# Layer 0 of a hybrid backbone: attention gates made a pair of tiles ahead, constants and some split weights kept in DRAM between the phases

## The chip, the cores and the metric

The kernel runs on one core of a Trainium2 chip. The metric is the device time of one execution in microseconds (us), the median of several runs. The engines are TensorE (PE; its weight loads are shown as PEld), VectorE (DVE), ScalarE (ACT), GpSimd (POOL) and SyncE (SP), whose queue issues the DMAs.

## The reference, cut to what matters

A latent stream of 2048 tokens and a context of 256 tokens, both 1024 wide, go through two layers. Every layer is a pre-RMSNorm sub-layer with shift, scale and gate rows that come from a conditioning vector. Layer 0 has one input projection that feeds two branches, and one output projection:

```python
u, v, ga, q, k, vv, gb = _split(h @ w_in, AB_SIZES)
ya = chunk_gmlp(gelu(u), gelu(v), ln_g, ln_b, w_s, b_s) * silu(ga)
yb = window_attention(q, k, vv, kc, vvc, sink) * silu(gb)
y = concatenate([ya, yb], axis=-1) @ w_out
```

`chunk_gmlp` applies a group layer norm to v and mixes the 128 positions of a chunk with a 128 x 128 matrix for each of 4 groups (`w_s`), adds `b_s` and multiplies by u. The attention has windows of +-128 tokens, the context as a prefix and a sink. Layer 1 is a bidirectional RG-LRU: a convolution of width 4, block-diagonal gates with biases and a decay that contains softplus(-lam), one scan in each direction, a SiLU gate and an output projection. A last RMSNorm gives the output.

## The kernel before

There are 18 tiles of 128 tokens (2 of context, 16 of latents), in 9 pairs. All is float32. For matmuls every operand is split into a high part that PE takes in one pass and a low part, the rest (`split`: the high part by a copy, on ACT unless said otherwise, and the low part by a subtraction, on DVE unless said otherwise); `mm3` multiplies high by high, low by high and high by low. A weight "unit" is half of the contraction of a block of 512 columns, or all of it for 256 columns: 2 MB with both parts. It is loaded in two halves of 0.5 MB through `raws`, six buffers of 4 KB a partition, and split (`unit_halves`). A "kept" half (`keep_halves`) is loaded, split and stored in DRAM with both parts; later one transfer of 1 MB (`kept_half`) brings it ready.

The program has four parts, which follow each other on the engines' queues.

1. The attention stage, a loop of steps `s` over tiles (18 and three more for the pipeline to drain). Each step makes one tile's norm, its transposed h (stored in DRAM as `h0s`), q, k and v, and the scores, softmax and values of an earlier tile, in four quarter steps that `merge` interleaves. One piece of other work from the list `mg_at` goes into a quarter step, from quarter step MOD_AT on: pieces of the conditioning rows (`mod_half`, tiles mraw, macc and msum) and kept halves of layer 1's weights. The tail (`tail_q`), in the last three steps, computes some of the ga and v projections ahead and loads weights `wu` 2 to 4.
2. The projection phase (the block of `c2`): u and v of a tile (`part_v`, `part_u`: matmuls pvv and pu), layer norm, the spatial product of a pair (`pair_b`: matmuls sv, tile ub), stored as `yas`. At its start `consts` loads and transposes the spatial weights (wsT) and 92 rows of small constants (cv) on PE, and computes softplus (tiles spt and sps). Weights for the next phase are split along the way.
3. The output phase (the block of `c3`): for a pair of tiles, `gate_b` loads the attention's outputs (ot) and the pair's h (one buffer, hp3), computes the SiLU gate by 96 matmuls pg of 256 columns and makes ybT; `y_rows` loads ya and transposes it on DVE (yT, 128 blocks of 32 x 256 over the phase), and its split gives yaT. `out_a` computes the output of one tile by 48 matmuls po of 512 columns (first the 12 on yaT, then 12 on ybT, for either half), the residual (xt) and the next layer's norm; its `fin`, called one tile later, transposes the new rows on DVE (h1T; on PE from tile 14 on), modulates them and stores them as `h1s`.
4. Layer 1, whose order on PE, ACT and DVE is written out by hand.

In the first three parts the order on each engine's queue comes from a planner that simulates the program: what comes first in the program, or is marked with a high priority, goes first where it is ready by the planner's own times. Each engine then runs its queue in order. Buffers of a phase lie where those of the phase before it lay; a tile waits for the last reader of what it covers.

In the order of the program the output phase before reads as follows, with `yaT` in one buffer and `ybT` in two:

```python
gated = gate_b(0); rows = [y_rows(0)]
for pr in range(NPAIR):
    split(yaT...)                        # pair pr, low part on POOL but for pr 0
    if pr == 0: wo.extend(...)           # the last two output weights: load and split
    for x in range(2):
        f = out_a(2 * pr + x, yaT, ybT); if pend: pend(); pend = f
        if x == 0 and pr + 1 < NPAIR:
            gated = gate_b(pr + 1); rows.append(y_rows(pr + 1))
```

## Time and profile before

| what | value |
|---|---|
| median of 3 runs | 2016.53 us (2014.89 to 2018.07) |
| the profiled execution, its own time | 2019.23 us |
| its span, first to last instruction | 2017.4 us |
| mean granted TensorE clock | 0.974 of full speed |
| PE busy | 1903.2 us (94%) |
| DVE busy | 1527.7 us (76%) |
| ACT busy | 1086.5 us (54%) |
| POOL busy | 619.8 us (31%) |

Busy time of an engine is the time in which it executes an instruction; matmuls overlap, so that the time from start to start is what one costs, and not its duration. A row of waits names the waiting engine and tile, and behind the arrow what it waited for last. The chain of waits follows the work that ended last back from releaser to releaser. All times count from the first instruction. "Granted clock" is the share of PE's full clock (2.4 GHz) that the chip allowed; its lower level is half of that.

### The profile page before, as it was taken

What the parts mean: (1) busy time and instruction counts of PE and PEld (TensorE: products, weight loads), DVE (VectorE), ACT (ScalarE), POOL (GpSimd) and SP (SyncE); (2) the same over time, 40 slices, a digit from 0 to 9 for tenths busy, and PEclk for the clock granted to TensorE, in tenths of its full rate; (3) what the DMA queues carried; (4) which work ended last, traced back from release to release, by engine and by line L of the source; (5) the groups of instructions that cost most, each with busy time, mean ns of one, the idle gap of its engine ahead of it and who ended that gap; (6) DMA issues with size and microseconds to landing.
All of it is one profiled execution on the core that took longest, in us unless ns stands there. A gap on an engine that the chain in (4) does not pass through costs nothing.

```text
span 2017.4 us, 33905 instructions
## 1 busy us (share of the span) xinstructions
PE 1903.2 (94%) x12159; PEld 1701.9 (84%) x12159; DVE 1527.7 (76%) x3223; ACT 1086.5 (54%) x2205; POOL 619.8 (31%) x801
## 2 busy tenths in 40 slices
PE   7999999999999899799989999999999999988998
PEld 3778888888887788688878889999999999877777
DVE  8878989786745787838888854798987566877863
ACT  6656656666655332323443551676767666756621
POOL 2745646454422311200010010443422121244310
PEclk8999999999999899899999999999999999988999
DMA  9355535352344897465555555324476464866442
GB/s 344 124 180 186 176 137 176 118 199 71 126 142 149 297 353 281 172 230 182 198 205 182 206 208 186 107 100 147 167 260 222 161 200 167 295 218 192 136 160 91
DMA packets 184788, 375.79 MB, mean 186 GB/s; under 512 B 18694, under 2 KB 78858, under 8 KB 176428
## 3 DMA queue, kind: packets, MB, share of 16 engines
q1 hardware_dynamic: 184620, 373.64, 53.0%
q8 instruction: 95, 1.56, 0.3%
q14 instruction: 73, 0.60, 0.1%
HBM read 246.41 MB, written 127.17 MB: 185 GB/s over the span
## 4 chain that ended last, share of the span: by engine, by line
PE 57%; DVE 19%; ACT 10%; DMA 7%; issue 6%; POOL 1%; SPq 1%; POOLq 0%; DVEq 0%; ACTq 0%
PE px L90 6%; PE px L92 6%; PE px L91 6%; DVE h1T L904 4%; PE pu L90 3%; PE pu L91 3%; PE pu L92 3%; PE po L573 3%; PE ptp L561 2%; DVE yT L904 2%; DVE macc L231 2%; ACT h1T L175 2%; DMA mraw<-in_w_mod 2%; PE pl L515 1%; PE pq L91 1%
## 5 line engine op out<-in xcount | busy, mean ns | idle before, releaser
L90 PE MATMUL px<-op,w 128*128 128x256 f32 x1088 | 308.1, 283 | 0.0
L91 PE MATMUL px<-op,w 128*128 128x256 f32 x1088 | 307.9, 283 | 0.0
L92 PE MATMUL px<-op,w 128*128 128x256 f32 x1088 | 307.9, 283 | 0.0
L91 PEld LDWEIGHTS px<-op,w 128*128 128x128 f32 x1088 | 208.9, 192 | 0.0
L90 PEld LDWEIGHTS px<-op,w 128*128 128x128 f32 x1088 | 208.9, 192 | 0.0
L92 PEld LDWEIGHTS px<-op,w 128*128 128x128 f32 x1088 | 208.9, 192 | 0.0
L543 POOL TENSOR_SCALAR s<-s,ri 128x640 f32<-128x640 f32 (+2 forms) x144 | 134.4, 947 | 97.1 <-DVE ri L540 93.0
L535 ACT ACTIVATE s<-s,mn 128x641 f32<-128x641 f32 (+2 forms) x144 | 113.3, 788 | 65.8 <-DVE mn L517 57.7
L84 ACT ACTIVATE pT<-ptp 128x512 fp32r<-128x512 f32 (+1 forms) x192 | 99.7, 536 | 89.5 <-PE ptp L561 86.4
L1108 POOL TENSOR_TENSOR ig<-ig,zf 128x512 f32<-128x512 f32 x72 | 109.9, 1534 | 98.0 <-ACT ig L1106 88.7
L87 DVE TENSOR_TENSOR zhl<-zf,zhl 128x512 fp32r<-128x512 f32 x72 | 60.2, 843 | 102.8 <-ACT zhl L84 102.7
L573 PE MATMUL po<-pT,v 128*128 128x256 f32 x656 | 130.1, 296 | 6.1 <-DVE pT L87 4.4
L87 DVE TENSOR_TENSOR pT<-ptp,pT 128x512 fp32r<-128x512 f32 (+1 forms) x192 | 114.4, 604 | 23.3 <-ACT pT L84 22.6
L90 PE MATMUL px<-w,op 128*128 128x512 f32 x256 | 103.5, 404 | 14.9 <-ACT px L1240 14.9
L573 PEld LDWEIGHTS po<-pT,v 128*128 128x128 f32 x656 | 98.5, 189 | 17.2 <-DVE pT L87 9.1
L175 ACT ACTIVATE h1T<-h1T,mc 128x128 f32<-128x128 f32 x112 | 44.7, 482 | 119.0 <-DVE h1T L904 119.0
L561 PE MATMUL ptp<-ident,s 128*128 128x128 f32 x656 | 104.0, 273 | 3.9 <-POOL s L543 2.1
L1152 POOL COPY carry<-T 128x2 f32<-128x2 f32 x68 | 34.7, 510 | 232.1 <-DVE T L1149 222.1
L904 DVE STREAM_TRANSPOSE h1T<-hrow 32x256 f32<-32x256 f32 x224 | 97.7, 436 | 8.1 <-ACT hrow L956 5.0
L91 PE MATMUL px<-w,op 128*128 128x512 f32 x256 | 102.5, 400 | 0.0
L92 PE MATMUL px<-w,op 128*128 128x512 f32 x256 | 102.4, 400 | 0.0
L517 DVE CUSTOM_DVE_ANT_0 s<-pl,mask,mn 128x384 f32<-128x384 f32 (+1 forms) x128 | 76.1, 594 | 31.5 <-PE pl L515 30.1
(280 smaller groups left out, 6237.4 us busy)
## 6 DMA issues: line engine op xcount, KB each, us to landing
hp<-h0s SPq DMA_DIRECT2D x45, 1024.0 KB
op<-h1s SPq DMA_DIRECT2D x64, 512.0 KB
mraw<-in_w_mod SPq DMA_DIRECT2D x48, 512.0 KB
h0s<-hT SPq DMA_DIRECT2D x18, 1024.0 KB
h1s<-h1hl SPq DMA_DIRECT2D x36, 512.0 KB
xt<-in_x SPq DMA_DIRECT2D x32, 512.0 KB
gs<-gs SPq DMA_DIRECT2D x64, 256.0 KB
raw<-in_ab_w_in SPq DMA_DIRECT2D x22, 512.0 KB
```

The source lines that it names most:

```text
L84: act.activation(hi, src, AF.Copy)
L87: (eng_lo or dve).tensor_tensor(lo, src, hi.bitcast(F32), ALU.subtract)
L90: pe.matmul(ps, lhsT=lhs(0), rhs=rhs(0), start=first, stop=False)
L91: pe.matmul(ps, lhsT=lhs(1), rhs=rhs(0), start=False, stop=False)
L92: pe.matmul(ps, lhsT=lhs(0), rhs=rhs(1), start=False, stop=last)
L175: act.activation(hT[:, o], tp[:, i], AF.Identity, scale=mc[:, 1, k, m:m + 1], bias=mc[:, 0, k, m:m + 1])
L535: act.activation(s[:, 0:nk], s[:, 0:nk], AF.Exp, scale=-1.0, bias=st["mn"][:, row, i:i + 1], accum_out=st["sm"][:, i:i + 1])
L543: pool.tensor_scalar(s[:, 1:nk], s[:, 1:nk], ri[:, i:i + 1], 0.0, ALU.mult, ALU.add)
L561: pe.transpose(tp[:, x, h], s_t[h][:, 1 + i * P:1 + (i + 1) * P], ident)
L573: pe.matmul(pos[t, g][:, 2 * P * e:2 * P * (e + 1)], lhsT=vl, rhs=pT[:, hl, x], start=i == 0 and hl == 0, stop=i == n - 1 and hl == 1)
L904: dve.transpose(out[o, :, s], src[s, :, o])
L1108: pool.tensor_tensor(res[1], res[1], zfs.pop((d, i, b)), ALU.mult)
```

## The change

- Output phase: the gates of pair `pr + 1` are made in the program before both outputs of pair `pr` (before: between the two). The split of ya has its low part on DVE for every pair (before: on POOL but for the first); the rows of the pair after it are loaded and transposed behind the split. For the first pair the ya split comes first of all, and both its gates and those of the second pair come ahead of the first output. The second pair's h goes to four of the six raw buffers in eight transfers; the other pairs keep the one hp3 buffer.
- The output projection's last two weights (four halves) and weights 4 and 5 of the input projection (four halves) are split as kept halves in the attention stage and come ready by 1 MB transfers. Both before were loaded and split where they were needed (4 in the tail, 5 at the start of the projection phase).
- The constants (spatial weights, the 92 columns, softplus) are made in three pieces at the head of the attention stage's list of pieces, stored in DRAM, and loaded behind it by three transfers. The list begins two quarter steps earlier (MOD_AT 6) and has 63 pieces instead of 52; the kept halves are spread evenly in it.
- h of the first two tiles of the projection phase is loaded during the attention tail, into a weight buffer.

The diff, cut to its core:

```diff
@@ constants @@
-MOD_AT = 8
+MOD_AT = 6
@@ new, at the head of the program @@
+    wsd = dram.tile([P, 2, 4, P], F32, name="wsd")
+    cvd = dram.tile([P, 92], F32, name="cvd")
+    spd = dram.tile([P, 3, 16], F32, name="spd")
+    def const_pieces(bank):
+
+        st = {}
+
+        def spatial():
+            wsr = raws.tile([P, 4, P], F32, tag="raw", name="wsr")
+            sp.dma_start(wsr, a["a_w_s"][0].rearrange("g p q -> p g q"))
+            wsT = raws.tile([P, 2, 4, P], F32R, tag="raw", name="wsT")
+            tp = bank([P, 4, P], "wstp")
+            for g in range(4):
+                pe.transpose(tp[:, g], wsr[:, g], ident)
+            split(wsT[:, 0], wsT[:, 1], tp)
+            sp.dma_start(wsd, wsT.bitcast(F32))
...
+            tpc = bank([P, 92], "cvtp")
+            pe.transpose(tpc, cr, ident[0:92, 0:92])
+            v = st["v"] = raws.tile([P, 256], F32, tag="raw", name="cols")
+            dve.tensor_copy(v[:, 0:92], tpc)
...
+            sp.dma_start(spd, o)
+
+        return [spatial, columns, softplus_neg]
@@ attention stage @@
-                    w, st[0] = unit_halves(pool_, wu_cols(i), act, (pool, dve))
+                    if i < 4:
+                        w, st[0] = unit_halves(pool_, wu_cols(i), act, (pool, dve))
+                    else:
+                        w = pool_.tile([P, 2, KT // 2, 512], F32R, tag="w", name="w")
+                        st[0] = lambda h: kept_half(w, ("wu", i), h)
+        hp01 = []
+
+        def load_hp01():
+            hp01.append(wb0.tile([P, 2, 2, KT, P], F32R, tag="w", name="hp01"))
+            for t in range(2):
+                sp.dma_start(hp01[0][:, t].bitcast(F32), h0s[t])
+
+        tail_q.insert(len(tail_q) * 2 // 3, load_hp01)
...
+        keep = [lambda i=i, h=h: keep_halves(("wu", i), wu_cols(i), h) for i in range(4, 6) for h in range(2)] + keep
+        keep += [lambda i=i, h=h: keep_halves(("wo", i), wide(a["ab_w_out"][0], 512, i), h) for i in range(2) for h in range(2)]
+        mg = const_pieces(mod_bank)
         for n, group in enumerate(groups):
-            mg += group + keep[3 * n // 2:3 * (n + 1) // 2]
+            mg += group + keep[len(keep) * n // 8:len(keep) * (n + 1) // 8]
@@ projection phase @@
+    sp.dma_start(cv[:, 0:92], cvd)
+    sp.dma_start(sps, spd)
...
+        for t in range(2):
+            hps[t] = hp01[:, t]
+        w = next_w().tile([P, 2, KT // 2, 512], F32R, tag="w", name="w")
         with tc.high_priority():
-            load_h(0)
-        load_h(1)
-        wu = wus + [unit_w(wu_cols(5), act, (pool, pool))]
+            for h in range(2):
+                kept_half(w, ("wu", 5), h)
+        wu = wus + [w]
         part_g(0)
+        wsT = b1.tile([P, 2, 4, P], F32R, name="wsT")
+        sp.dma_start(wsT.bitcast(F32), wsd)
...
-            if t == 0:
-                wsT, bs = consts()
@@ output phase, gate_b @@
-            hp = b1.tile([P, 2, 2, KT, P], F32R, tag="hp3", name="hp3")
-            for x in range(2):
-                sp.dma_start(hp[:, x].bitcast(F32), h0s[2 * pr + x])
+            if pr == 1:
+                hps_ = []
+                for q in range(4):
+                    hps_.append(raws.tile([P, 2, 2, 2, P], F32R, tag="raw", name="hp3"))
+                    for x in range(2):
+                        sp.dma_start(hps_[q][:, x].bitcast(F32), h0s[2 * pr + x][:, :, 2 * q:2 * q + 2])
+
+                def rows_of(hl, k):
+                    return hps_[k // 2][:, :, hl, k % 2]
+            else:
+                hp = b1.tile([P, 2, 2, KT, P], F32R, tag="hp3", name="hp3")
+                for x in range(2):
+                    sp.dma_start(hp[:, x].bitcast(F32), h0s[2 * pr + x])
+
+                def rows_of(hl, k):
+                    return hp[:, :, hl, k]
...
-                            lambda hl: hp[:, :, hl, k], k == 0, k == KT - 1)
+                            lambda hl: rows_of(hl, k), k == 0, k == KT - 1)
@@ output phase, the loop @@
+        def y_halves(raw, lo):
+            yaT = b1.tile([P, 2, 2, 4, P], F32R, tag="yaT3", name="yaT3")
+            split(yaT[:, 0], yaT[:, 1], raw, eng_lo=lo)
+            return yaT
+
         pend = None
-        gated = gate_b(0)
-        rows = [y_rows(0)]
+        halves0 = y_halves(y_rows(0), dve)
+        gated = [gate_b(0)]
+        for i in range(2):
+            wo.append(next_w().tile([P, 2, KT // 2, 512], F32R, tag="w", name="w"))
+            for h in range(2):
+                kept_half(wo[-1], ("wo", i), h)
         for pr in range(NPAIR):
-            ybT = gated
-            raw = rows.pop(0)
-            yaT = b1.tile([P, 2, 2, 4, P], F32R, tag="yaT3", name="yaT3")
-            split(yaT[:, 0], yaT[:, 1], raw, eng_lo=pool if pr else dve)
-            if pr == 0:
-                wo.extend(unit_w(wide(w_out0, 512, i), act, (pool, dve)) for i in range(2))
+            if pr + 1 < NPAIR:
+                gated.append(gate_b(pr + 1))
+            ybT = gated.pop(0)
+            yaT = y_halves(rows, dve) if pr else halves0
+            if pr + 1 < NPAIR:
+                rows = y_rows(pr + 1)
...
-                if x == 0 and pr + 1 < NPAIR:
-                    gated = gate_b(pr + 1)
-                    rows.append(y_rows(pr + 1))
```

## Rows read from the trace of the kernel before

**Rows 1.** Busy time by stage (PE, PEld, DVE, ACT, POOL; clock, DMA share, GB/s).

```profile
0.00:654.00 654.00, 617.24 (x3821) 525.72 (x3822) 515.69 (x1302) 402.16 (x872) 317.61 (x439) 0.99 0.47 164
...
902.00:1163.00 261.00, 243.88 (x1349) 212.01 (x1348) 224.45 (x433) 108.81 (x210) 27.02 (x35) 0.96 0.55 196
...
860.00:865.00 5.00, 4.37 (x21) 3.83 (x20) 0.00 (x0) 0.00 (x0) 0.00 (x0) 0.53 1.03 406
```

**Rows 2.** Timeline of PE, attention to projections (start, length, instruction, idle before).

```profile
655.70 0.66 PE L736 MATMUL wstp<-ident,wsr 128*128 128x128 f32 x4 [1.40 <-DVE o L584]
...
662.70 0.79 PE L90 MATMUL pvv<-w,hp 128*128 128x512 f32 x1 [2.17 <-DMA hp<-h0s]
...
664.15 0.63 PE L90 MATMUL pvv<-w,hp 128*128 128x512 f32 x1
664.58 0.63 PE L91 MATMUL pvv<-w,hp 128*128 128x512 f32 x1
```

**Rows 3.** Timeline of PE in the output phase, about 1003 us.

```profile
1002.80 0.28 PE L91 MATMUL pg<-hp,w 128*128 128x256 f32 x1
...
1003.74 0.40 PE L90 MATMUL po<-w,yaT 128*128 128x512 f32 x1
...
1006.52 0.39 PE L90 MATMUL po<-w,ybT 128*128 128x512 f32 x1
```

**Rows 4.** What PE waited for, 836 to 880 us (total, times, longest).

```profile
PE po L91 <- DVE yaT L87: 8.6, 1, 8.6
PE sv L90 <- DVE ub L836: 4.7, 1, 4.7
```

**Rows 5.** The chain of waits, projections to outputs (start, length, what).

```profile
838.75 2.72 DVE w L87
841.47 2.77 DVE ub L788
...
851.12 9.95 DMA hp<-h0s
...
861.97 0.21 PE pg L92
```

**Rows 6.** What PE waited for in the steady output phase.

```profile
PE po L90 <- ACT yaT L84: 17.1, 6, 4.2
```

**Rows 7.** The instructions that write yaT: shortest, median and longest ns; starts.

```profile
L84 ACT ACTIVATE yaT<-yT x8: 1039/1042/1060, 902.4 to 1162.7; 128x1024 fp32r<-128x1024 f32 x8
L87 POOL TENSOR_TENSOR yaT<-yT,yaT x8: 2372/2388/2412, 903.6 to 1163.8; 128x1024 fp32r<-128x1024 f32 x8
```

**Rows 8.** The instructions on yraw: the first pair's low part.

```profile
L87 DVE TENSOR_TENSOR yaT<-yraw,yaT x1: 1226/1226/1226, 854.2 to 854.2; 128x1024 fp32r<-128x1024 f32 x1
```

**Rows 9.** Groups of DVE instructions, 902 to 1163 us (busy, mean ns, idle before).

```profile
L87 DVE TENSOR_TENSOR h1hl<-h1T,h1hl 128x512 fp32r<-128x512 f32 x26 | 26.7, 1028 | 13.3 <-ACT h1hl L84 12.8
...
L87 DVE TENSOR_TENSOR ybT<-sg,ybT 128x512 fp32r<-128x512 f32 x14 | 9.6, 688 | 10.7 <-ACT ybT L84 10.7
```

**Rows 10.** What DVE waited for, 880 to 1160 us.

```profile
DVE ybT L87 <- ACT ybT L84: 13.3, 7, 2.5
DVE h1hl L87 <- ACT h1hl L84: 12.8, 14, 1.1
```

**Rows 11.** Busy time in two stretches of the attention stage, columns as rows 1.

```profile
180.00:420.00 240.00, 231.27 (x1492) 202.80 (x1492) 215.48 (x557) 155.39 (x342) 136.03 (x173) 1.00 0.47 161
460.00:540.00 80.00, 79.32 (x533) 71.25 (x532) 58.71 (x164) 55.29 (x123) 38.11 (x59) 1.00 0.30 108
```

**Rows 12.** The low part of a kept half on DVE.

```profile
L87 DVE TENSOR_TENSOR whl<-raw,whl x20: 1195/1224/3043, 99.6 to 757.3; 128x1024 fp32r<-128x1024 f32 x20
```

**Rows 13.** One of the small operations of softplus on DVE.

```profile
L762 DVE TENSOR_TENSOR spt<-spt,spt x9: 174/174/176, 663.1 to 666.4; 128x16 f32<-128x16 f32 x9
```

**Rows 14.** Timeline of SP: two stores of h in the attention stage.

```profile
277.27 0.34 SPq L384 DMA_DIRECT2D h0s<-hT  x1
313.56 0.34 SPq L384 DMA_DIRECT2D h0s<-hT  x1
```

79 lines of the change are left out of this document (35 added, 44 removed).

## The prediction, before the result was known

> **What bounds the kernel now.** I read the table of stages first. In the attention stage TensorE (PE) is busy 617 of 654 us and VectorE (DVE) 516; in the steady part of layer 0's output phase, 902 to 1163 us, PE has 244 of 261 us and DVE 224, at a granted clock of 0.96 [rows 1]. PE sets the pace nearly everywhere, so time can only come out of places where PE waits or runs at the lower of its two clock levels. The waits of PE and its timeline name three such places.
>
> First, the step from attention to the u/v projections. The gMLP weights' transposes start at 655.70, and the first projection matmul only at 662.70, after a transfer of h. Then PE is at the lower clock: two starts 0.43 us apart [rows 2], where the same shape later takes 0.232 (1003.74 to 1006.52, twelve matmuls) [rows 3].
>
> Second, the step from projections to outputs. PE waits 4.7 us for the last DVE product on u and 8.6 us for the low half of ya [rows 4]. The chain of waits tells why: a weight split of 2.72 us on DVE, a product of 2.77 us behind it, then the transfer of the first pair's h from 851.12, 9.95 us long; the first gate matmuls after it step by 0.21 us [rows 5], not 0.1175 (1002.80 to 1003.74, eight of them) [rows 3].
>
> Third, the steady output phase: 17.1 us in six waits of the output matmuls for the high half of ya on ScalarE (ACT) [rows 6]. These halves are made at 902.4 for the second pair of tiles and at 1162.7 for the ninth [rows 7], seven periods of 37.2 us. A pair holds 96 gate and 96 output matmuls: 96 x 0.1175 + 96 x 0.232 = 33.5 us [rows 3]. So 3.7 us of every period, 26 us in all, is wait or lower clock.
>
> **A, the attention stage: added work, +2.5 us.** Eight halves of weights (units 4 and 5 of the input projection, two of the output projection) are now split here and stored, each with one load of 0.5 MB, two stores of 0.5 MB, a split on ACT and one on DVE of 1.22 us [rows 12]; three pieces for the constants come before them, the third of which is thirty small DVE operations of about 0.174 us [rows 13], 5.2 us. One piece goes into a quarter step: 52 before, 63 after, so eleven more quarter steps of 654 / 21 / 4 = 7.8 us carry one. What does a piece cost PE? From 180 to 420 us, where each quarter step has one, PE is idle 8.7 of 240 us (3.6%); from 460 to 540, without, 0.7 of 80 (0.9%) [rows 11]. The difference, 2.7% of 86 us, is 2.4 us. Bounds: 0, since PE keeps the pace there, and 8 x 1.22 + 5.2 + some 2 = 17 us if all that DVE work were serial. I take 2.5, by the windows, which hold just such pieces.
>
> **B, from attention to projections: -7.5 us.** The h tiles of the first two rows and unit 4 come during the attention tail, unit 5 comes as ready halves, and the constants' transposes, their copies and the small DVE chain leave this place. Two small loads (92 and 48 columns) and one of 0.5 MB take their place; the first reader of the last is the spatial product, behind three pairs of projections. PE then needs only a free bank and starts where the transposes did, at 655.70: 7.0 us earlier [rows 2]. Nine matmuls at the lower level cost 9 x (0.43 - 0.23) = 1.8 us more now; I let part of that go. What is late next is unit 5's 2 MB: the two transfers of like size took 9.95 us [rows 5]; issued at about 656, where h is issued now, they land at 666, while the first u matmul would want them at 655.7 + 24 x 0.232 = 661.3. That wait of 4.7 us gives the poor bound, -3; the good one is -8.8.
>
> **C, from projections to outputs: -5 us.** The last two output weights (four halves) are no longer split here. That removes four ACT passes, two POOL and two DVE subtractions, the 2.72 us one on the chain among them; the u product behind it should fall as well, as should the 4.7 us wait [rows 4, 5]. The split of ya for the first pair comes before the second pair's transposes, and 22 us of gate matmuls (two pairs) stand ahead of its reader, which covers the 8.6 us. Lost now: 4.7 + 8.6, plus 12 matmuls of 512 columns and 22 of 256 at the lower level, 12 x 0.2 + 22 x 0.1 = 4.6; together 17.9. Lost after: PE is through at about 841 and then has nothing but the gates, which want 2 MB of h. I put their issue at 842 (SP's queue no longer waits there for the split that frees raw buffers) and their landing 9.95 us later, at 852: 11 us idle and some 2 at the lower level, 13. The difference is 5. On SP's queue come besides: four ready halves of 1 MB, the second pair's h in eight transfers of 0.25 MB, and the loads of attention outputs and ya. The four loads have the first output tile's second half as their reader, 28 us on. Bounds: if h is issued at 836, with the last layer norm, 7 us are lost and C is -11; if the 4 MB of weights go ahead of it, they add at least 4 MB / 406 GB/s = 9.9 us [rows 1] and C is +5.
>
> Here the Trainium skill (DMA: Bandwidth & Descriptors, Specifications) speaks against the change: it puts a core's limit at HBM at some 358 GB/s. By that the 9 MB due before the second pair's gates are done would take 25 us, against 22 at the row's rate, and C would be about -2. The trace moved 406 GB/s in that very place, so the measurement decides.
>
> **D, the steady output phase: -15 us.** Gates of the next pair now stand ahead of both outputs of a pair, so between the last reader of the old ya halves and the first of the new lie 11.3 us of gate matmuls. The split needs ACT's 1.04 us and DVE's 1.23 us [rows 7, 8], and fits. It leaves POOL, where it took 2.39 us [rows 7]. While POOL did it, DVE was slow: h1hl subtractions mean 1.03 us, the same shape for ybT 0.69 [rows 9]. That excess, 26 x 0.34 = 8.8 us over 261, is 1.26 us a pair, just the 1.23 us that DVE takes over. DVE's load stays at 224.45 / 261 x 37.2 = 32.0 us a pair [rows 1], 96% of a period of 33.5. DVE also idles 13.3 and 12.8 us behind ACT for ybT and h1hl [rows 10], 3.7 us a pair, and not all of that will be filled. I take a period of 35.3: 7 x 1.9 = 13.3 us, and 2 us for the step at either end. Bounds: 7 x 3.7 = 26 and 0. The last pair has no gates left to cover its split; there the hidden-row transposes on PE stand in, as they do now.
>
> **The sum.** +2.5 - 7.5 - 5 - 15 = -25 us. Inside the projection phase PE has no gaps worth the name, and layer 1 (from 1196 us) is untouched but for two small loads in place of computed columns: 0 each. The profiled execution took 2019.2 us (span 2017.4), 2.7 above the median of the runs, 2016.5. From the median: **1991.5 us**.
>
> **Rivals.** *DVE becomes the bound of the output phase.* For: 32.0 us of load and 3.7 of waits on ACT give 35.7, and one late product stalls everything behind it in order; against: four PSUM banks, 22 us of output matmuls, lie between. Period 36.7, D = -4: 2003.
>
> *The first gates wait behind weights.* For: the weights' buffers come free when the last u matmul ends, so their loads can be issued before those of h; C = +5 and the time 2001.5. The skill's rule (DMA: Bandwidth & Descriptors, Queues, rings and completion order) is that each DMA engine consumes descriptors in ring order; by it h would land behind all 4 MB. No row here shows the two loads together.
>
> *Everything goes.* A 0, B -8.8, C -11, D -24: -44, 1973.
>
> *Slower: the added pieces stretch the attention steps.* Each keeps three of six raw buffers until its stores have landed, and the front of each step (which needs a raw buffer for h) waits for them. Two stores of h lie 36.3 us apart at the worst (277.27 and 313.56) [rows 14], against a mean step of 654 / 21 = 31.1. If each of the eight halves stretched a step by that 5.2 us, A would be 42 and the time 2031; it decides from 27.5 / 8 = 3.4 us a piece. Against: the twelve halves already there leave PE idle only 3.6% [rows 11].
>
> *It does nothing*: where the planner that lays out these phases orders PE as before, the waits move and the sum stays within 4 us. The changed program order speaks against it.
>
> **How the numbers follow.** What a measurement of this kernel can tell from no change is about 0.2%, 4 us. Forecast (1981 to 1998) 0.47; DVE bound or gates behind weights (1998 to 2011) 0.26; everything (below 1981) 0.13; nothing 0.06; slower 0.08. The first three are faster: 0.86. The range reaches over the first two and into the third, to 1975, and up to 2011; 0.17 is left out.
>
> **What would show it.** B: the first pvv matmul 6 to 8 us sooner after the last attention matmul, and no wait there for h. C: no 4.7 us wait of sv, gates of two pairs ahead of the first output matmul, the first gate 10 to 14 us after the last sv. D: no wait of po for ya on ACT, POOL nearly idle, h1hl near 0.7 us, a period of 34.5 to 36. A: the end of attention at 654 to 660. Wrong would be: attention ending after 665, pg or po waiting for DVE in each pair, or the first gate later than 20 us after sv.

## The result, and the profile after

The changed kernel takes 2028.85 us (median of 6 runs, 2024.34 to 2037.65), the kernel before 2016.71 beside it (6 runs, 2014.89 to 2018.07): a ratio of 1.0065, 95% interval 1.0044 to 1.0086. It is slower; the prediction said 1991.5, 1975 to 2011.

The profiled execution of after is the lowest of its six (2024.34, span 2022.5), so its trace can show 5.1 us of the 12.1 between the medians (the span of before is 2017.4). These 5.1 fall on the stages as follows, by the timelines of PE.

| | before | after | difference |
|---|---|---|---|
| last attention matmul ends | 654.3 | 675.4 | +21.1 |
| from there to the first projection matmul (pvv) | 8.4 | -0.2 | -8.6 |
| from there to the last spatial matmul (sv) | 183.4 | 180.5 | -2.9 |
| from there to layer 1's first matmul (px) | 343.9 | 340.0 | -3.9 |
| layer 1, to the end of the span | 827.4 | 826.8 | -0.6 |

The busy time by stage in the kernel after (columns as in [rows 1]: PE, PEld, DVE, ACT, POOL; clock, DMA share, GB/s), to be held against [rows 1, 11]:

```profile
0.00:675.00 675.00, 628.81 (x3826) 535.18 (x3827) 524.54 (x1346) 410.54 (x884) 308.10 (x439) 0.97 0.54 188
180.00:420.00 240.00, 230.50 (x1470) 201.79 (x1469) 207.09 (x545) 156.62 (x343) 125.53 (x170) 0.99 0.50 172
460.00:540.00 80.00, 76.58 (x500) 67.74 (x499) 61.07 (x170) 52.72 (x115) 37.18 (x58) 0.98 0.44 153
891.00:1170.00 279.00, 263.31 (x1449) 227.16 (x1448) 235.16 (x468) 121.20 (x227) 11.09 (x30) 0.98 0.54 198
```

In attention PE is idle 46 us where it was 37. That is 9 of the 21 us; the other 12 are PE's busy time (628.8 for 617.2 us, five instructions more), at a mean granted clock of 0.97 where it was 0.99: about half of the growth is matmuls at the lower level. From 460 to 540, where before had no pieces and lost 0.7 of 80 us, PE now loses 3.4. POOL is nearly out of the output phase, as planned.

The step from attention to projections on PE's timeline (start, length, instruction, idle before), against [rows 2]:

```profile
674.76 0.63 PE L632 MATMUL po<-pT,v 128*128 128x256 f32 x3 [0.47 <-DVE pT L87]
675.23 0.40 PE L90 MATMUL pvv<-w,hp 128*128 128x512 f32 x1
675.46 0.39 PE L91 MATMUL pvv<-w,hp 128*128 128x512 f32 x1
```

The projections start without a wait and at once at the higher clock, 0.23 us from start to start. What PE waited for from 836 to 900 us, and then from 900 to 1190, against [rows 4, 6]:

```profile
PE pg L90 <- DMA hp<-h0s: 15.0, 1, 15.0
...
PE po L91 <- DVE yaT L87: 9.2, 4, 3.5
PE tp L1022 <- ACT hrow L1006: 6.5, 1, 6.5
```

The 4.7 us of sv, the 8.6 and 17.1 us of po are gone. In their place the first pair's gates wait 15.0 us for h, the output matmuls 9.2 us for DVE, and the last pair's transposes 6.5 us for ACT. The halves of ya and a hidden row's low part (shortest, median and longest ns; starts), against [rows 7, 9]; the last row is the kernel before:

```profile
L84 ACT ACTIVATE yaT<-yT x8: 1042/1042/1061, 910.7 to 1168.7; 128x1024 fp32r<-128x1024 f32 x8
L87 DVE TENSOR_TENSOR yaT<-yT,yaT x8: 1221/1225/1226, 915.7 to 1169.8; 128x1024 fp32r<-128x1024 f32 x8
...
L87 DVE TENSOR_TENSOR h1hl<-h1T,h1hl x27: 682/686/696, 925.4 to 1162.9; 128x512 fp32r<-128x512 f32 x27
...
L87 DVE TENSOR_TENSOR h1hl<-h1T,h1hl x26: 684/693/2466, 924.8 to 1154.0; 128x512 fp32r<-128x512 f32 x26
```

The subtraction of a hidden row took 1.03 us in the mean before: five of the 26 ran beside POOL's subtraction and took 2.44 to 2.47 us, the others about 0.69. Without POOL all take 0.69. The second pair's outputs start at 924.6, 9 us after its low half began; the ninth pair's at 1170.5, 0.7 us after. A lead of 8 us has been used up on the way.

### The profile page after: what moved, and what is told of

It reads as the page before. It is cut to its first block, busy times and chain, and to the rows that moved or that the text cites. A ratio compares the mean times of both kernels' runs of the same rounds, so it can differ in the third digit from the quotient of the medians.

```text
span 2022.5 us, 33966 instructions
## 1 busy us (share of the span) xinstructions
PE 1907.2 (94%) x12159; PEld 1706.1 (84%) x12159; DVE 1510.8 (75%) x3236; ACT 1087.1 (54%) x2205; POOL 582.1 (29%) x788
## 4 chain that ended last, share of the span: by engine, by line
PE 56%; DVE 20%; DMA 7%; ACT 7%; issue 6%; POOL 1%; SPq 1%; DVEq 0%; ACTq 0%; POOLq 0%
PE px L90 6%; PE px L91 6%; PE px L92 6%; DVE h1T L940 5%; PE pu L90 3%; PE pu L91 3%; PE pu L92 3%; PE po L632 2%; DVE yT L940 2%; DMA mraw<-in_w_mod 2%; PE ptp L620 2%; DVE macc L231 2%; PE pr L90 1%; PE pr L91 1%; PE pr L92 1%
## 5 line engine op out<-in xcount | busy, mean ns | idle before, releaser
L163 POOL TENSOR_SCALAR ms<-ss 128x1 f32<-128x1 f32 x36 | 11.5, 320 | 381.8 <-ACT junk L161 375.0
L1208 POOL COPY carry<-T 128x2 f32<-128x2 f32 x68 | 33.5, 493 | 234.2 <-DVE T L1205 224.4
L90 PE MATMUL pr<-zhl,w 128*128 128x256 f32 x288 | 83.6, 290 | 16.8 <-ACT r L1162 16.8
```

The lines of the kernel that those rows point to most:

```text
L90: pe.matmul(ps, lhsT=lhs(0), rhs=rhs(0), start=first, stop=False)
```

## The experiments

Eighteen kernels ran besides the change. The times are medians with the ratio to the kernel before on the same chip; "attention" is the end of the last attention matmul in the profiled execution (654.3 before, 675.4 after), "outputs" the time from the last sv to the first px (343.9 and 340.0).

| run | attention | pvv | outputs | time | ratio, interval |
|---|---|---|---|---|---|
| list_two_earlier | 663.0 | 674.6 | 339.6 | 2029.3 (one run) | |
| kept_halves_alone | 670.3 | 683.8 | 348.7 | 2041.5 | 1.0122, 1.0104 to 1.0141 |
| no_kept_halves | 668.2 | 668.0 | 337.9 | 2020.5 | 1.0023, 1.0009 to 1.0037 |
| two_raw_buffers | 666.7 | 666.5 | 340.4 | 2021.6 | 1.0027, 1.0014 to 1.0041 |
| list_where_it_was | 664.9 | 664.7 | 340.9 | 2021.1 | 1.0030, 1.0018 to 1.0042 |
| two_raw_and_list | 662.7 | 662.5 | 339.6 | 2019.4 | 1.0004, 0.9991 to 1.0017 |
| early_h_alone | 655.1 | 654.9 | 342.2 | 2013.0 | 0.9986, 0.9969 to 1.0002 |
| first_pair_in_raw | 680.6 | 680.4 | 340.7 | 2033.1 | 1.0081, 1.0064 to 1.0098 |
| weights_behind_gates | 678.9 | 678.7 | 340.0 | 2031.7 | 1.0074, 1.0054 to 1.0095 |
| output_order_alone | 655.9 | 664.2 | 339.7 | 2014.7 | 0.9984, 0.9973 to 0.9995 |
| order_and_last_gates_late | 654.6 | 662.9 | 336.9 | 2012.1 | 0.9983, 0.9970 to 0.9995 |
| rows_on_pe_earlier | 678.0 | 677.9 | 336.1 | 2028.8 | 1.0052, 1.0032 to 1.0073 |
| order_late_two_raw | 652.0 | 664.4 | 336.5 | 2011.6 | 0.9979, 0.9968 to 0.9990 |
| order_late_early_h_two_raw | 650.8 | 650.7 | 336.7 | 2001.4 | 0.9931, 0.9913 to 0.9950 |
| order_early_h_rows_on_pe | 652.0 | 651.8 | 334.7 | 2000.1 | 0.9912, 0.9896 to 0.9929 |
| fast_and_constants | 662.3 | 662.1 | 337.6 | 2009.6 | 0.9962, 0.9951 to 0.9974 |
| fast_and_kept_halves | 666.3 | 666.1 | 340.3 | 2012.7 | 0.9974, 0.9962 to 0.9987 |
| change_repaired | 663.0 | 662.8 | 339.0 | 2016.0 | 0.9982, 0.9970 to 0.9994 |

One trace stands behind each stage time, and one program does not repeat its stages exactly. The changed kernel and three runs that edit only its output phase (rows_on_pe_earlier, first_pair_in_raw, weights_behind_gates) issue the same instructions in the same order in attention, and end it at 675.4 to 680.6. Layer 1, whose order no run edits, takes 822.0 to 830.3 us. list_two_earlier, whose output phase is not edited, has 339.6 for "outputs" and the kernel before 343.9. So a difference of less than some 5 us in one of these stages is not told by one trace.

### Why attention grew by 21 us

First what the trace of after shows. The chain of waits through one loss (start, length, what), 471 to 481 us:

```profile
471.84 0.96 ACT whl L84
...
472.82 0.33 SPq L130
...
473.20 5.44 DMA mraw<-in_w_mod
...
478.66 0.48 DVE macc L229
479.15 0.61 DVE hT L87
...
479.81 0.38 PE pk L91
```

ACT finishes the high part of a kept half; only then SP can issue its store (L130), and behind that store in SP's queue stands the load of a modulation weight. It lands at 478.66; DVE has been waiting 2.3 us for it and has the low part of hT queued behind, which PE needs. PE loses 2.0 us, and the next 10 us have a mean granted clock of 0.83 (480 to 490): for part of them PE is at its lower level, with 0.21 us between matmuls of 256 columns where it was 0.12. Here the piece costs through two queues, and not as work. What DVE waited for at these loads, 60 to 676 us, in the kernel before, after, and with two raw buffers:

```profile
DVE macc L229 <- DMA mraw<-in_w_mod: 6.7, 4, 4.4
```

```profile
DVE macc L231 <- DMA mraw<-in_w_mod: 8.0, 5, 2.4
DVE macc L229 <- DMA mraw<-in_w_mod: 6.5, 5, 2.3
```

```profile
DVE macc L231 <- DMA mraw<-in_w_mod: 1.1, 1, 1.1
DVE macc L229 <- DMA mraw<-in_w_mod: 0.4, 1, 0.4
```

And what SP waited for at the stores of halves, attention from 180 us on, in before, after and with two raw buffers:

```profile
SPq L130 <- ACT whl L84: 19.1, 8, 4.3
```

```profile
SPq L130 <- ACT whl L84: 29.9, 14, 5.9
```

```profile
SPq L130 <- ACT whl L84: 18.7, 7, 4.7
```

Two of the experiments ask for the change of one line. **list_two_earlier** is the kernel before with `MOD_AT = 6`, **list_where_it_was** the changed one with `MOD_AT = 8`:

> The kernel before with its list of pieces begun two quarter steps earlier (MOD_AT 6 instead of 8) and nothing else: not one operation more. If the loss in the attention stage is an accident of any new layout of the planner's order, its end moves by 5 us or more from 654 here too. If it comes from the added work, the end stays within 3 us of 654 and the waits of DVE for mraw within 3 us of the 6.7 before.

> The changed kernel with the list of side pieces beginning at its eighth quarter step again, not its sixth; every operation of the change stays. If the place where the list begins is what costs attention time beside the shortage of raw buffers (the kernel before lost 8.7 us of attention by that line alone), the last attention matmul ends at 664 to 670 us instead of 675.4 and the time falls to 2018 to 2023. If the added pieces themselves cost it, wherever the list begins, attention ends within 2 us of 675.4 and the time stays at 2026 to 2031.

The line alone costs the kernel before 8.7 us of attention, with no operation more (one execution); in the changed kernel it gives back 10.5. That is what the first run's first theory said: a new layout of the planner's order is enough. And it is mostly the clock. The whole stage in list_two_earlier, against [rows 1], and in list_where_it_was, against the first row after:

```profile
0.00:663.00 663.00, 623.78 (x3822) 531.25 (x3822) 512.33 (x1302) 401.75 (x872) 312.48 (x439) 0.97 0.47 162
```

```profile
0.00:664.90 664.90, 619.63 (x3828) 526.68 (x3829) 527.79 (x1346) 409.50 (x883) 306.28 (x439) 0.99 0.55 191
```

PE's idle time changes by 2.4 and 0.9 us (36.8 to 39.2, 46.2 to 45.3), its busy time by 6.5 and 9.2. The waits above do not rank the runs either. SP's for halves in list_where_it_was, as above:

```profile
SPq L130 <- ACT whl L84: 41.3, 13, 6.6
```

With that, and 10.6 us of DVE's waits for the loads, it ends attention at 664.9; two_raw_buffers, below, has 18.7 and 1.5 and ends it at 666.7. These waits are one way in which time is lost, not the account of it.

**two_raw_buffers** (changed kernel; a piece holds two raw buffers, not three):

```diff
-        hl = [raws.tile([P, kh, n], F32R, tag="raw", name="whl") for _ in range(2)]
+        hl = [raws.tile([P, kh, n], F32R, tag="raw", name="whl"), raw.bitcast(F32R)]
```

> The changed kernel, but every kept half writes its low part over the loaded weights, so that it holds two of the six raw buffers and not three; same instructions, sizes and transfers. If the late loads of the attention stage come from the raw buffers that the kept halves hold, the stage ends at 655 to 664 instead of 675, DVE waits under 8 us for mraw instead of 14.5, and the time falls by 8 to 15 us, to 2014 to 2021. If buffers don't matter (added transfers and splits as such, or the accident of the order), the stage ends at 670 or later and the time stays within 6 us of 2029.

Attention ends 8.7 us sooner, with the waits for the loads down from 14.5 to 1.5 us; both its end and its time lie just outside the first theory's figures. This edit changes the planner's order too, so it does not part the buffers from the layout. **two_raw_and_list** makes both edits:

> The changed kernel with two raw buffers a side piece (low part over the raw weights) and the list beginning at its eighth quarter step: both attention experiments at once. If these are two causes, their gains add: the last attention matmul ends at 655 to 659 us (675.4, less 8.7 and 10.5) and the time is 2012 to 2016. If both only ease one shortage, attention ends at 663 to 667 and the time is 2019 to 2022.

The two gains of 8.7 and 10.5 do not add to 19.2: together they give 12.7 us, so they overlap for the most part, as the second theory said; 8.4 us of the 21.1 stay. The equal-work comparison (matmuls added up at their full-clock cost, and the times compared at which two kernels reach the same sum) says where: with both edits the loop is only 1.5 us behind before up to 622 us, and most of the rest is lost in the last 30 us of the stage. The change itself is by the same sums not behind at 350 us, 6 us behind at 400, 11 at 500, 13 at 622 and 19 at the stage's end: it loses in a few places, not a little with each piece. The windows of the last 30 us, before, after, in list_two_earlier, and in the fast version without added pieces:

```profile
624.00:654.00 30.00, 26.56 (x179) 22.61 (x178) 20.92 (x61) 19.09 (x40) 7.85 (x15) 1.00 0.37 116
```

```profile
645.00:675.00 30.00, 20.96 (x127) 17.56 (x126) 23.56 (x51) 18.59 (x34) 11.72 (x12) 0.89 0.56 180
```

```profile
633.00:663.00 30.00, 24.36 (x154) 20.69 (x152) 20.40 (x57) 18.24 (x38) 7.84 (x15) 0.89 0.34 110
```

```profile
620.00:650.00 30.00, 24.86 (x171) 21.20 (x170) 22.85 (x60) 20.18 (x40) 11.16 (x16) 1.00 0.54 173
```

After, PE is busy 21 of 30 us at a clock of 0.89. In that stretch stand, of the splits and gain products of weights for later phases, thirteen instructions of 17.4 us on DVE, ACT and POOL; before there were two of 2.3 us (two_raw_and_list has sixteen of 20.4). The planner has laid side work of the next phases into attention's tail. One such place in the timeline of after, DVE and then PE:

```profile
658.41 2.48 DVE L125 TENSOR_TENSOR raw<-raw,kgain 128x1024 f32<-128x1024 f32 x1
660.82 0.68 DVE L87 TENSOR_TENSOR pT<-ptp,pT 128x512 fp32r<-128x512 f32 x1
```

```profile
661.64 1.08 PE L620 MATMUL ptp<-ident,s 128*128 128x128 f32 x4 [2.67 <-DVE pT L87]
```

The gain product of a later weight, 2.48 us long, stands ahead of the softmax's low part, and PE waits 2.67 us. But the fast version has eight such instructions of 10.8 us in its last 30 us, and PE is busy there 1.7 us less than before, at the full clock. list_two_earlier has the two of the kernel before and has 2.2 us less of busy time and a clock of 0.89. So neither is such work needed for a loss in the tail, nor does all of it cost one; that the changed kernel's loss comes from it is read from single waits like this one, and a tail without it was not tried.

Which added pieces cost, the constants or the halves? **kept_halves_alone** is the kernel before with the eight kept halves and nothing else, **no_kept_halves** the changed kernel without them (the weights are split where they were):

```diff
+        keep = [... keep_halves(("wu", i), wu_cols(i), h) for i in range(4, 6) for h in range(2)] + keep
+        keep += [... keep_halves(("wo", i), wide(a["ab_w_out"][0], 512, i), h) for i in range(2) for h in range(2)]
...
```

> The kernel before plus the eight kept halves alone (their loads where the changed kernel has them); constants, early h and output phase as before. Theory 1 (kept halves): the attention stage ends at 668 to 680, DVE waits 10 us or more for mraw, time 2022 to 2035. Theory 2 (constants): it ends at 652 to 658 and the time is 2008 to 2016, since the split work is gone from the two steps between phases. Theory 3 (accident of the order): anything from 650 to 680 without more waits for mraw.

> The changed kernel without its eight new kept halves: weights 4 and 5 of the input projection and the last two output weights are loaded and split where they are needed, as before the change; constants, early h and the order of the output phase stay as changed. Theory 1 (the kept halves hold raw buffers, so the loads of the pieces in the attention stage land late, and DVE and ACT wait for them in order): the attention stage ends by 660 us instead of 675, DVE waits for mraw under 6 us in all instead of 14.5, and the time is 2010 to 2016. Theory 2 (the constants' pieces do it): the attention stage still ends after 668, time 2024 or more. Theory 3 (any edit lays the planner's order out anew, and the loss is an accident of that): the end may lie anywhere from 650 to 680, without DVE waiting less for mraw.

By themselves the halves make attention 16.0 us longer and the kernel 1.2% slower (in the trace also 5.1 us in the step behind attention and 4.8 in the outputs). Without them the change is nearly even, but attention still ends at 668.2 and DVE waits 10.6 us for the loads, where the first theory wanted 660 and under 6. None of the three theories fits whole: the time is under the second's 2024, and the waits are less than the 14.5 that the third would leave. Added one kind at a time to the fast version below (650.8; list at 8, two raw buffers):

> The fast version (order, late last gates, early h, two raw buffers; 2001.4, attention ends at 650.8) with the change's three constant pieces and none of the added kept halves. If the kept halves are what costs, attention ends at 650 to 654 and the time is 1998 to 2003, since the constants' work leaves the place ahead of the outputs. If the constants at the list's head cost, attention ends at 657 or later and the time is 2007 or more.

> The fast version with the eight added kept halves (units 4 and 5 of the input projection, two of the output projection) and none of the constant pieces. If the kept halves cost, attention ends at 658 to 663 and, with the four ready halves of 1 MB that come ahead of the first pair's h, the time is 2009 to 2015. If the constants cost, attention ends at 651 to 655 and the time is 1999 to 2004.

Neither theory alone holds: both kinds cost. The constants lengthen attention by 11.5 us, the halves by 15.5; each shortens the projection phase by 5 (187.3 to 182.4 and 182.2 us), so that work did leave it. The sum is 8.2 and 11.3 us slower by the medians, which are of different chips; by the ratios it is some 0.3% and 0.4%. That the pieces cost is shown by this. How much of it is their work and their buffers, and how much the new order and the clock, is not: no run adds a piece and keeps the order.

### From attention to the projections

**early_h_alone**: the kernel before with h of the first two rows loaded in the tail.

```diff
+            hp01.append(wb0.tile([P, 2, 2, KT, P], F32R, tag="w", name="hp01"))
...
+        tail_q.insert(len(tail_q) * 2 // 3, load_hp01)
```

> The kernel before, with nothing of the change but the h tiles of the first two rows loaded into a weight buffer during the attention tail. The prediction's part B says that the first projection matmul then waits for no h: if the transfer is what the 7 us behind attention wait for, it starts 4 to 7 us sooner after the last attention matmul and the time is 2010 to 2013. If it then waits as long for something else that stands there (unit 5's weights, the constants' transposes and copies), or the planner puts that work into attention's tail instead, the sum moves by less than 2 us: 2014.5 to 2018.

pvv starts with the last attention matmul's end, 7.8 us sooner, and attention is not longer. 4.7 us of it are lost again in the projection phase (188.1 against 183.4), where unit 5's weights and the constants still stand. The time falls by 3.8 us, to the edge of the first theory's figures; its interval just includes no change.

### From the projections to the outputs

SP's timeline in after (start, length, instruction):

```profile
840.12 4.62 SPq L960 DMA_DIRECT2D hp<-h0s  x6
...
849.10 3.61 SPq L134 DMA_DIRECT2D w<-keptwo  x4
856.52 0.33 SPq L871 DMA_DIRECT2D yas<-ub  x1
...
857.86 0.91 SPq L967 DMA_DIRECT2D hp<-h0s  x2
```

The second pair's h goes first and its gates run from 850.7; the first pair's h is issued at 857.86, behind 4 MB of weights and a store that waits for DVE, and its gates start at 872.77. All that while the DMA engines are full (850 to 875 us):

```profile
DMA packets 2582, 9.65 MB, mean 386 GB/s; under 512 B 229, under 2 KB 229, under 8 KB 2325
```

**first_pair_in_raw** gives the four raw buffers to the first pair, not the second; **weights_behind_gates** puts the weights' loads behind the second pair's gates in the program:

```diff
-            if pr == 1:
+            if pr == 0:
                 hps_ = []
```

> The changed kernel, but the first pair's h goes to the four raw buffers and the second pair's to the one hp3 buffer, the other way round. If the 15 us wait of the first gates comes from hp3 standing behind the weights and the last ya store on SP's queue while raw buffers were free earlier, the wait falls to under 6 us and the time drops by 6 to 10 us against the changed kernel, to 2016 to 2022. If the transfers themselves are the limit (9 MB in that place), only the name of the pair that waits changes, and the time stays within 4 us of 2029.

> The changed kernel, but the four loads of ready output weights (4 MB) stand in the program behind the second pair's gates instead of ahead of them. If the 15 us wait of the first gates comes from h standing behind these weights on SP's queue and in the transfers, it falls to under 7 us and the time by 6 to 12 us, to 2017 to 2023. If h is held by its buffer or by the ya stores, the wait stays above 11 us and the time within 4 us of 2029.

Neither helps, as the second theory of each said: the wait is 16.1 and 15.4 us (the first run's 2033.1 lies just above that theory's figures). In the second, the planner still issued the weights ahead of h, since the first pair's h stood behind the store. What does shorten it is to have no kept output weights: 6.7 us in no_kept_halves, 7.0 in output_order_alone, 8.4 in fast_and_constants, against 14.9 to 16.5 in all that have them with the new order (kept_halves_alone, with the old order, waits 5.1 for h and 1.7 for the weights). But there the output weights are split beside the projections again, sv waits 4.0 us for ub, and the outputs stage gains 2 to 3 us (337.9 against 340.0; 337.6 against 340.3), less than the spread.

### The output phase

The periods, from the first output matmul of one pair to that of the next, are in after 33.5, 33.5, 33.5, 33.5, 38.2, 35.7, 39.7 and 31.7 us. The windows of the second and the eighth (columns as in [rows 1]):

```profile
925.00:958.00 33.00, 33.00 (x191) 28.84 (x191) 28.41 (x58) 14.39 (x29) 0.73 (x2) 1.00 0.56 207
...
1139.00:1170.00 31.00, 23.52 (x102) 18.91 (x102) 27.46 (x52) 17.89 (x33) 1.57 (x4) 0.94 0.41 150
```

Four periods run at PE's floor, on a lead: the second pair's ya was transposed from 856 us on, while PE waited for h. DVE itself does not keep that pace. Its low halves of ya start at 915.7, 952.6, 989.9, 1027.1, 1064.3, 1101.6 and 1138.8: 37.0 to 37.2 us apart. Of the lead of 8.9 us each period takes 3.7, and after the third it is gone. One of DVE's periods, in after and (37.9 us) before, and the two idle times that fill most of the rest in after, over six of them:

```profile
954.40:991.60 37.20, 37.20 (x225) 33.00 (x225) 32.30 (x66) 16.23 (x32) 1.46 (x4) 1.00 0.54 199
```

```profile
944.50:982.40 37.90, 34.30 (x186) 29.65 (x185) 33.12 (x66) 15.81 (x31) 3.84 (x5) 0.93 0.50 183
```

```profile
L940 DVE STREAM_TRANSPOSE h1T<-hrow 32x256 f32<-32x256 f32 x192 | 83.7, 436 | 18.6 <-ACT hrow L1006 16.0
...
L87 DVE TENSOR_TENSOR h1hl<-h1T,h1hl 128x512 fp32r<-128x512 f32 x24 | 15.9, 688 | 8.1 <-ACT h1hl L84 7.9
```

DVE is busy 32.3 of 37.2 us and waits 4 for ACT, for the hidden row and for its high part; before it was 33.1 of 37.9. The eighth window holds no gates, 22.3 us of output matmuls, and takes 31. The chain of waits just there runs on DVE, with the low half of ya between the block transposes (start, length, what):

```profile
1136.26 0.44 DVE h1T L940
...
1138.80 1.22 DVE yaT L87
...
1141.87 0.44 DVE yT L940
```

**output_order_alone** is the kernel before with the output phase's order (gates ahead, split of ya on DVE, second pair's h in raw buffers). **order_and_last_gates_late** adds to it that the last pair's gates stand between the eighth pair's two output tiles again:

```diff
-            if pr + 1 < NPAIR:
+            if pr + 1 < NPAIR - 1:
                 gated.append(gate_b(pr + 1))
...
+                if x == 0 and pr == NPAIR - 2:
+                    gated.append(gate_b(pr + 1))
```

> The kernel before plus the new order of the output phase alone (gates a pair ahead, low part of ya on DVE, second pair's h in raw buffers); the last two output weights are loaded and split there as before. The attention stage must end as before, at 654. If the output phase gains in its middle what it gives back at both ends (15 us wait of the first gates for h, 6.5 us wait of the last pair), its length changes by less than 6 us and the time is 2011 to 2021. If the new order is worth what was forecast (15 us in the steady part), the time is 1998 to 2006.

> The output phase's new order alone on the kernel before (as in output_order_alone, which took 2014.7), but the last pair's gates are made where they were, between the two outputs of the eighth pair. If the 9 us given back at the end of that phase come from the last pair having no gates to cover its split and its hidden rows, they stay: 2004 to 2008, with no wait of several us of tp for hrow. If DVE's backlog in the last pairs is what PE meets there, whatever stands between, the time stays at 2012 to 2017.

The order alone makes the kernel 0.16% faster, with the same late periods (37.2, 39.5 and 35.3 after four of 33.5). In the traces the late gates shorten outputs by 2.8 us, less than the spread: the 5.0 us for the hidden row go, and the eighth pair waits 6.0 us for ACT's half of ya instead. The two runs were not on the same chip, and between their ratios no difference can be told.

**rows_on_pe_earlier** takes the block transposes of tiles 10 to 13 from DVE (`T_PE = 14` to `10` in the changed kernel):

> The changed kernel with the hidden rows of row tiles 10 to 13 transposed on TensorE, as those of 14 to 17 are, not in 32x32 blocks on VectorE: 28 us less for VectorE in the seventh and eighth period, and 32 transposes more for TensorE (some 2 us). If VectorE is the bound (its instructions of one pair add up to 33.4 us, and it waits some 4 us a pair for ScalarE; the first four periods of 33.5 us only spend what it had done ahead), the periods of 35.7 and 39.7 us fall to 34 to 36, the waits of the output matmuls for the low half of ya go in those pairs, and from the first output matmul to layer 1 it takes 298 to 301 us instead of 304.6; the time is 2022 to 2026. If the halves are late for another reason, the periods stay at 36 to 40 and the time is 2028 to 2032.

From the first output matmul to px it takes 299.5 us (after: 304.6), and PE's wait for the low half of ya falls from 9.2 to 3.5 us. What DVE waited for, 1025 to 1190 us, in after and then here:

```profile
DVE h1T L940 <- ACT hrow L1006: 8.1, 3, 2.7
DVE h1hl L87 <- ACT h1hl L84: 6.2, 4, 2.2
DVE tmp L1000 <- PE po L92: 6.1, 2, 3.9
```

```profile
DVE tmp L1000 <- PE po L92: 17.3, 8, 4.1
DVE h1hl L87 <- ACT h1hl L84: 13.3, 5, 3.6
```

DVE now waits for PE, 17.3 us instead of 6.1: with 28 us less work it is no longer the bound for most of that stretch. But the single periods did not fall as the first theory said: after four of 33.5 they are 39.4, 43.4, 34.9 and 23.8 us, and the sixth holds a wait of 5.6 us of the transposes on PE for their hidden row, now in that pair. The time is that of the change and in the second theory's range: in this profiled execution attention, in the same order, ended 2.6 us later, and layer 1 took 3.5 longer, both within the spread.

### Versions

**order_late_two_raw**, **order_late_early_h_two_raw** and **order_early_h_rows_on_pe** put together, on the kernel before, the order with late last gates and two raw buffers; then early h; then tiles 12 and 13 on PE (`T_PE = 12`). **change_repaired** is all of the change with the list at 8, two raw buffers, late last gates and `T_PE = 12`.

> The changed order of the output phase with the last pair's gates behind the eighth pair's first output tile (that alone gave 2012.1), and every side piece with two raw buffers instead of three: its low part is written over the raw weights. In the changed kernel two buffers took 8.7 us off attention, where DVE's waits for loads fell from 14.5 to 1.5 us; here the list has 52 pieces and those waits are 8.7 us. If they cost PE as much each, attention ends 3 to 5 us sooner and the time is 2007 to 2010. If they only cost when 63 pieces fill the list, attention ends within 1.5 us of 654.6 and the time is 2011 to 2014.

> As the run beside it, and the first two rows' h loaded in the attention tail as well: none of the added pieces, none of the kept halves. If the gains of order, early h and two raw buffers stand in different places and add up, the time is 2001 to 2005. If the early h brings nothing, or the planner gives back in attention what it brings, the time is that of the run beside it within 2 us.

> The fastest version so far (order of the output phase with late last gates, early h, two raw buffers; 2001.4) with the hidden rows of tiles 12 and 13 on TensorE too: 14 us less for VectorE. If VectorE bounds the late periods, its sixth and seventh period (37.2 and 36.5 us) fall by 3 to 5 us together against some 1 us of transposes and the time is 1996 to 1999.5; if not, it is 2001 to 2003.

> Every part of the change, with two raw buffers a side piece, the list at its eighth quarter step, the last pair's gates late, and the hidden rows of tiles 12 and 13 on TensorE. If the causes found are all, it keeps attention within 5 us of the kernel before and gains behind it: 2004 to 2010. If the kept halves of the added weights cost more than they save, it stays behind the version beside it by over 5 us.

Two raw buffers alone bring attention 2.6 us, less than the spread, and the time nothing that can be told. Early h then brings 10 us (2011.6 to 2001.4), more than the 3.8 it brought to the kernel before; the stretch from pvv to sv loses 4.8 again, as there. The rows on PE add 1.4 us, within the spread; its interval (0.9896 to 0.9929) overlaps that of the run without them. Of the two periods that were to fall, the fifth went from 37.2 to 38.2 us and the sixth from 36.6 to 36.0. These two are the fastest versions, 0.7% to 0.9% below the kernel before, with none of the constants and none of the added kept halves. The repaired change stays 15.9 us behind the version beside it, on the same chip and with the same edits but for the constants and the kept halves: the second theory of that run holds for the added pieces as a whole, they cost more than they save. What PE waited for in the version of 2001.4, 640 to 900 us:

```profile
PE sv L90 <- DVE ub L845: 7.3, 3, 4.0
PE pg L90 <- DMA hp<-h0s: 7.2, 2, 4.9
```

## Why the prediction was wrong

**The sum.** Predicted were A +2.5, B -7.5, C -5 and D -15. In the traces attention grew by 21.1, the step behind it shrank by 8.6, the projections took 2.9 less, and C and D together gave 3.9 and not 20, no more than the spread of that stage.

**A, the failed step.** "I take 2.5, by the windows, which hold just such pieces." The mean idle share of a stretch that had pieces was used as the price of eleven more. Measured were 21.1: 9.4 of idle time and 11.6 of longer busy time, at a mean clock of 0.97 for 0.99. The price failed three times. It was read from stretches with a granted clock of 1.00 [rows 11] and had no term for the clock. It was spread evenly over the quarter steps, and the loss came in a few places, the last 30 us among them. And it left the earlier start of the list at nothing, which costs the kernel before 8.7 us of attention by itself. The bounds (0 and 17 us of DVE work) also left out that a piece's store can hold SP's queue until ACT has written a half, with the load of other work behind it; the trace shows that at 471 to 481 us, and how much of the whole it makes stays open.

The rival "the added pieces stretch the attention steps" had 0.08, and its time of 2031 is within 2.2 us of the median. That is luck: it had A at 42 us and the other three at -27.5. Its cause is half right at most: with a raw buffer less a piece attention ends 8.7 us sooner; but in the wait shown it was a modulation weight in SP's queue that came late, not h at a step's front.

**B, right.** pvv starts 8.6 us sooner after attention, without a wait, at the higher clock; unit 5's weights make PE wait 0.9 us, which the poor bound had put at 4.7. The 2.9 us that the phase itself took less had been given as 0. But alone (early h) the same gain costs no attention time; with the constants and the halves it is paid for ahead of it.

**C, half.** The 4.7 us of sv and the 8.6 of po went as predicted. By equal work the stretch gained 2.8 us (11.1 behind before its end, 8.3 after), between the forecast's -5 and the +5 of "the first gates wait behind weights". The mechanism is that rival's: the first pair's gates start 17.1 us after the last sv (855.7), not 10 to 14, behind the weights in the queue. "I put their issue at 842" failed for this pair: its h was issued at 857.9. The second pair's gates, which the planner put first, cover part of it; the prediction had not thought of the two pairs changing places. The rule of the Trainium skill (DMA: Bandwidth & Descriptors, Queues, rings and completion order), that each DMA engine consumes descriptors in ring order, agrees with the 14.9 to 16.5 us that PE waits for h in every kernel that has the new order and those weights ahead of h; no run has the same loads with h first. The 358 GB/s of the Trainium skill (the same page, Specifications) do not agree with the trace: 386 were moved over 25 us.

**D, its period mis-sized.** On PE the period's mean over the seven with gates is (1138.7 - 891.1) / 7 = 35.4 us, where 35.3 was taken, and POOL, h1hl and PE's waits on ACT came as written. That the number came out is luck: it is the mean of four periods on a lead and three without, and the lead is paid back at the end. The step that failed is "a period of 35.3", which left DVE 3.3 us of idle time beside 32.0 of work. The work came out (32.3 us); the idle time is 4.9, most of it behind ACT as before, and DVE's own period went from 37.9 only to 37.2. That is the rival "DVE becomes the bound", which had 36.7. "There the hidden-row transposes on PE stand in" failed with it: they wait 6.5 us for the row itself, which comes out of the chain on DVE that is late, and the eighth pair's 22.3 us of output matmuls take 31.7, a loss of 9.4.

**The median** is another 7 us above what the traces differ by; the profiled execution of after was its fastest. Where these lie is not shown by it, but the three runs with the same attention program ended attention 2.6 to 5.2 us later, so part of them may lie there.

## What to carry to other kernels

A piece of side work is not priced by its busy time, nor by the mean idle share of a stretch that has such pieces: look in the DMA-issuing queue for what stands behind its store and who waits for that load, count the buffers it keeps, and compare the granted clock of the stage as well as its idle time. A planner that orders by its own times can lay out the stage ahead of an edit anew, so that stage has to be read again after it, and one-line edits of position belong among the trials. In a phase where a second engine is near the bound, the first periods can run on a lead; read the period on that engine, from start to start of one of its instructions, and the last pair, which has nothing left to cover it. A stage's time from one trace has a spread: take it from kernels that run the same program there.

## What was not expected of the hardware

- The start of a list of small pieces, moved by two quarter steps without any operation more, changed the time from 2016.5 to 2029.3 us (one run); in attention, 6.5 of the 8.7 us were busy time of PE, at a clock of 0.97 for 0.99.
- A wait of PE of 2.0 us in attention was followed by 10 us with a mean granted clock of 0.83, part of them at the lower level; in the fast version's last 30 us, where no wait is that long, it was 1.00.
- DVE subtractions that ran beside a subtraction on POOL took 2.44 to 2.47 us, where the same shape takes 0.69 without it.
- One attention program, instruction for instruction, ended at 675.4, 678.0, 678.9 and 680.6 us in four kernels.
